# Gates of a gated hybrid block, projected in other pairs of column tiles and in another order among the pool's products

## The chip, the cores and the metric

One core of one Trainium2 chip runs the whole block: one decoder layer for a sequence of 1024 tokens of width 1024, in float32. The metric is the device time of one execution in microseconds, as the median of several runs. The profile is one more execution, recorded by the hardware profiler; its times count from the start of its span.

## The reference

```python
proj = x @ w_in            # 1024 x 1024 @ 1024 x 7168
q, f_pre, i_val, o_gate, pool_v, gate_a, gate_b = jnp.split(proj, ...)   # 1024 columns each
o = hgrn2_chunked(...)     # recurrence, 8 heads of 128
a = (rmsnorm(o) * g * sigmoid(o_gate)) @ w_a
b = (causal means of pool_v over 2, 4, 8, 16 tokens, minus pool_v) @ w_pool, in 4 groups of 256, * pool_scale
mix = (sigmoid(gate_a) * a + sigmoid(gate_b) * b) @ w_out
x = LN(alpha * x + mix);  x = LN(alpha * x + relu(x @ w_up)^2 @ w_down)
```

The change concerns the two projections gate_a and gate_b (columns 5 x 1024 and 6 x 1024 of w_in), their sigmoids, and the products of the pool, b.

## The kernel before

**Products.** The big products are made by a Strassen-like scheme. `pair` (L260) takes two column tiles of 128 columns of a weight matrix, each in an upper and a lower half of 512 rows: blocks b11 and b21 of the first column tile, b12 and b22 of the second. It makes the outputs of both column tiles for both halves of the tokens by seven products instead of eight. Each weight operand is split in a high and a low part (`split`, L117 on ScalarE, L118 on VectorE) and each of the seven products consists of twelve matmuls of 128 x 128 by 128 x 512 (L199 to L201: four blocks of rows, high times high, high times low, low times high). The products sum in three PSUM banks: p1 in the first, copied to SBUF (L268, tile c11) before p6, p5 and p3 go on in the same bank; p2 in the second; p7 and p4 in the third. The copies and sums (L268, L272) yield four results of 128 x 512: first column tile and first token half at p7, then the others at p5, p4 and p3. Each result is handed to a `take` function.

**Weights.** `w_blocks` (L206) fetches the blocks into two raw tiles, one for each half of the rows, of which there are two buffers in all: a pair fills both. If the second column tile directly follows the first in the matrix, a single DMA for each raw tile fetches 256 neighbouring columns, in rows of 1 KB (L214). Otherwise there is one DMA for each block, in rows of 512 bytes (L220).

**Tiles of the results.** `c_soon` hands out tiles of a ring with two buffers (c11, short-lived), `c_late` tiles of a ring with four (c21, c22 and the tile of the last sum). `c_tile()` of `o_sums` takes every third of its tiles from the first ring and the others from the second. A tile becomes free when the DMA that stores it has landed.

**The order of the work around the change.** For each head h and token half u there is a call of `hgrn` (L803), the recurrence, and around it the pairs that project the next heads' inputs and the output gates. A table, `EXTRAS` (L933), places further work behind each (h, u):

- `pooled(g)`: projection and causal means of pool group g, stored to DRAM (heads 0 to 3);
- `gates(j)` (L685): one pair of column tile j of gate_a and column tile j of gate_b, 1024 columns apart; a sigmoid on each of the four results (L693), each stored to DRAM (L696) as ga[j] and gb[j] for both halves of the tokens. The last, gates(7), uses the room tiles q, f, og and v instead of the two rings, since those have no user any more, and multiplies (L695) its two results for gate_b with the pool's products pb[7], which it loads, before it stores them as pb[7];
- `o_sums(kp)` (L602): loads four tiles of the normed recurrence outputs o (L591), adds and subtracts them (L605 to L608) and stores four sums (L610). They are operands of the merge. o_sums(3) is called with tiles of its own at the end of the last `hgrn`;
- `pool_products(g)` (L705): loads the group's weights (L713), four pooled tiles and the gates gb of its two column tiles, splits the weights and pooled tiles, makes 24 matmuls (L104 to L106), scales and gates the results out of PSUM on VectorE (L726) and stores them as pb (L727). For column tile 7 the gate isn't there yet; ScalarE scales the result alone (L724). Its tiles are ten room tiles: three q, three f, two og and two v, which is all of these rings; its weights take one of the two raw buffers.

Before, the table says for heads 4 to 7: gates(0) behind (4, 1); gates(1), o_sums(0) behind (5, 1); gates(2), o_sums(1) behind (6, 1); gates(3) behind (7, 0); and behind (7, 1) gates(4), o_sums(2), pool_products(0), gates(5), pool_products(1), gates(6), pool_products(2), pool_products(3), gates(7). The last `hgrn` runs at a raised priority.

Behind that comes the merge: `o_operand` (L594) loads o and the sums, pairs of w_a make a, and `gated` (L982) loads ga and pb and forms the gated sum.

The source's order isn't yet the order on the chip: a scheduler with a model of the time line (`schedule_with_timeline_sim=True`) lays out each engine's instructions at build, by the source's order, priorities and free tiles. Afterwards each engine works its list in order. All the DMAs named here are issued by SyncE (SP), also in order: an issue that waits for its tile or its data holds up those behind it.

Of the kernel before, what the change touches and what calls it, by code (L numbers as in the profile page):

```python
# [42 lines left out]
def tile_hybrid_block(  # L43
# [77 lines left out]
    def split_into(t, src):  # L121
# [9 lines left out]
        out=cmask, in_=cmask, compare_op=ALU.is_ge, fill=0.0, base=0,  # L131
# [93 lines left out]
    def loaded_blocks(*args):  # L225
        raw, load = w_blocks(*args)
        load(0, 1)
        return raw
# [20 lines left out]
    spare = []  # L249
# [7 lines left out]
    def c_late():  # L257
        return c_tile(False)
# [95 lines left out]
    def run(*pairs, made=(), behind=()):  # L354


        for i, steps in enumerate(zip(*pairs)):
            made_now = list(made[i]) if made else []
            if made_now:
                made_now.pop(0)()  # L360
            with tc.issue_after(made_last[behind[i]]) if behind and behind[i] else nullcontext():
                ws = [{operand: operand() for operand in operands} for operands, _ in steps]
            for n in range(len(ws[0])):
                if made_now:
                    made_now.pop(0)()
# [223 lines left out]
    def loaded(src, tile_of):  # L589
        t = tile_of()  # L590
        nc.sync.dma_start(out=t, in_=src)  # L591
        return t
# [22 lines left out]
    with tc.tile_pool(name="tmp", bufs=1, side="right", reuse_waits="tile") as tmp:  # L615
# [14 lines left out]
        def tt(tag, dtype=F32):  # L630
            pool = tmp if tag in ("q", "f", "og", "v") else hgp
            return pool.tile([P, HALF], dtype, tag=tag, name=nm(tag), bufs=RINGS.get(tag, 1))
# [35 lines left out]
            src = vd[u][h // CH].rearrange("p (c d) -> p c d", d=HALF)[:, :, h % CH * P : (h % CH + 1) * P]  # L668
            return loaded(src, lambda: tmp.tile([P, CH, P], F32, tag="v", name=nm("v"), bufs=RINGS["v"]))

        def output_gates(h):

            def take(dst, src=False):
                def put(t):
                    s = c_late() if src else t
                    A.activation(s, t, AF.Sigmoid)
                    nc.sync.dma_start(out=dst, in_=s)
                return put

            run(pair(  # L680
                loaded_blocks(w_in, 3 * D + h * P, 3 * D + (h + 1) * P), (c_soon, c_late, c_late),
                (take(ogd[h][0]), take(ogd[h + 1][0], True), take(ogd[h][1]), take(ogd[h + 1][1])),
            ))

        def gates(j):  # L685
            spare = j == KT - 1
            rooms = [lambda tag=tag: tt(tag) for tag in ("q", "f", "og")] if spare else (c_soon, c_late, c_late)

            def take(dst, src=None, more=None):
                def put(t):  # L690
                    s = (tt("v") if spare else c_late()) if src else t
                    more_of = loaded(more, lambda: tt("v")) if more is not None else None
                    A.activation(s, t, AF.Sigmoid)  # L693
                    if more_of is not None:
                        V.tensor_mul(s, s, more_of)  # L695
                    nc.sync.dma_start(out=dst if more is None else more, in_=s)  # L696
                return put

            more = pbd[j] if spare else (None, None)
            run(pair(  # L700
                loaded_blocks(w_in, 5 * D + j * P, 6 * D + j * P), rooms,
                (take(gad[j][0]), take(gbd[j][0], True, more[0]), take(gad[j][1]), take(gbd[j][1], False, more[1])),
            ))

        def pool_products(g):  # L705

            tags = iter(("q", "f", "og", "v") * 3)

            def room(dtype=F32):
                return tt(next(tags), dtype)  # L710

            raw = raw_tile().rearrange("p k n c -> p (k n c)")[:, : 2 * 2 * P].rearrange("p (k c) -> p k c", c=2 * P)
            nc.sync.dma_start(out=raw, in_=w_pool[g].rearrange("(k p) c -> p k c", p=P))  # L713
            wh, wl = split(raw, lambda: room(F32R).rearrange("p (k c) -> p k c", c=2 * P))
            for u in range(2):
                pl = [split(loaded(pod[2 * g + i][u], room), row_tile) for i in range(2)]
                for i in range(2):
                    w = slice(i * P, (i + 1) * P)
                    j = 2 * g + i
                    t = room() if j == KT - 1 else loaded(gbd[j][u], room)  # L720
                    ps = ps_tile()
                    mm3(ps, [(wh[:, c, w], wl[:, c, w], *pl[c]) for c in range(2)])
                    if j == KT - 1:
                        A.activation(t, ps, AF.Copy, scale=pscale[:, j : j + 1])  # L724
                    else:
                        V.scalar_tensor_tensor(t, ps, pscale[:, j : j + 1], t, ALU.mult, ALU.mult)  # L726
                    nc.sync.dma_start(out=pbd[j][u], in_=t)  # L727

        def pooled(g):
# [73 lines left out]
        def hgrn(h, u, ft, q, v, og, state):  # L803
# [139 lines left out]
        for h in range(HEADS):  # L943
            fs, qs = nxt
            state = None
            for u in range(2):
                v, og = values(h, u), loaded(ogd[h][u], lambda: tt("og"))
                with tc.high_priority(PRIO_LAST) if (h, u) == (HEADS - 1, 1) else nullcontext():
                    state = hgrn(h, u, fs[u], qs[u], v, og, state)
                    if (h, u) == (HEADS - 1, 1):  # L950
                        tags = iter(("tD", "tE", "tF", "tC"))
                        o_sums(h - CH, lambda: tt(next(tags)))
                if h + 1 < HEADS and u:
                    nxt = head_inputs(h + 1)
                    if h % 2:
                        output_gates(h + 1)
                for what, j in EXTRAS.get((h, u), ()):
                    dict(gates=gates, pooled=pooled, pool_products=pool_products, o_sums=o_sums)[what](j)


        hg_scope.close()
# [436 lines left out]
```

## Time and profile before

| | |
|---|---|
| median of 3 runs | 1461.44 us (1459.88 to 1463.6) |
| the profiled execution, its own time | 1460.58 us |
| its span | 1458.8 us |
| PE (matmuls) busy | 1437.8 us, 99% |
| VectorE, ScalarE busy | 1138.1 us, 754.6 us |
| mean rate of the DMAs | 155 GB/s |

PE stands for TensorE's matmuls and PEld for its weight loads, DVE for VectorE, ACT for ScalarE, SPq for the queue of SyncE. A group or an instruction is named by its line, its engine, its operation, and `out<-in` by the program's tile names: `ga<-c` stores a result tile as ga, `q<-gb` loads a gate into a room tile. A bracket behind an instruction of the timeline holds the idle time of its engine before it and what ended that.

### The profile page before, as it was taken

How to read it: one execution, taken by the hardware profiler on the slowest of the kernel's cores; microseconds unless marked ns; L12 is line 12 of the kernel's file. 1: busy time of each engine (PE TensorE's matmuls, PEld its weight loads, DVE VectorE, ACT ScalarE, POOL GpSimd, SP SyncE). 2: the span in 40 equal slices, each digit the busy share in tenths (PEclk: the TensorE clock that was granted, in tenths of full speed). 3: DMA queues.
4: the chain of work that ended last, by engine and by line, in shares of the span. 5: the costliest groups of instructions: out<-in, count | busy, mean ns of one | idle time of the engine just before them, and what ended most of it. 6: DMA issues, size and time to landing. Idle time of an engine off the chain costs nothing.

```text
span 1458.8 us, 20894 instructions
## 1 busy us (share of the span) xinstructions
PE 1437.8 (99%) x7505; PEld 1183.8 (81%) x7505; DVE 1138.1 (78%) x1838; ACT 754.6 (52%) x1383; POOL 65.6 (4%) x244
## 2 busy tenths in 40 slices
PE   9999999999999999999999999999999999999997
PEld 7888888887888888777888878888888888888886
DVE  5967989899998795768985597666666787777977
ACT  5445566565556566355442376555555443433535
POOL 0002010011000020000002100000000100000000
PEclk9999999999999999999999999999999999999999
DMA  7242233323233547987563235445464874444422
GB/s 253 66 130 87 88 102 102 94 88 109 95 109 109 172 126 238 345 289 248 197 223 119 73 96 193 154 139 169 143 242 152 285 261 146 158 146 158 130 73 116
DMA packets 160616, 226.84 MB, mean 155 GB/s; under 512 B 11232, under 2 KB 84480, under 8 KB 160512
## 3 DMA queue, kind: packets, MB, share of 16 engines
q1 hardware_dynamic: 158576, 218.93, 44.9%
q0 software_dynamic: 1152, 4.19, 0.8%
q10 hardware_dynamic: 784, 2.38, 0.6%
q8 instruction: 59, 0.97, 0.3%
q14 instruction: 45, 0.37, 0.1%
HBM read 154.16 MB, written 71.30 MB: 155 GB/s over the span
## 4 chain that ended last, share of the span: by engine, by line
PE 87%; DVE 5%; DMA 4%; ACT 2%; issue 1%; SPq 0%; DVEq 0%; ACTq 0%
PE ps_pj L199 15%; PE ps_pj L201 14%; PE ps_pj L200 14%; PE ps_pj L1280 4%; PE ps_pj L1281 4%; PE ps_pj L1279 4%; PE ps_pj L104 2%; PE ps_pj L105 2%; PE ps_pj L106 2%; PE ps_tr L1279 1%; PE ps_tr L1281 1%; PE ps_tr L1280 1%; DMA raw<-in_w_in_dram 1%; PE sc L887 1%; PE ps_sc L199 1%
## 5 line engine op out<-in xcount | busy, mean ns | idle before, releaser
L199 PE MATMUL ps_pj<-act,w 128*128 128x512 f32 x1068 | 419.6, 395 | 5.9 <-ACT c L268 3.6
L200 PE MATMUL ps_pj<-act,w 128*128 128x512 f32 x1068 | 416.8, 391 | 0.5 <-DVE act L123 0.5
L201 PE MATMUL ps_pj<-act,w 128*128 128x512 f32 x1068 | 412.5, 392 | 0.1
L199 PEld LDWEIGHTS ps_pj<-act,w 128*128 128x128 f32 x1068 | 200.5, 188 | 51.4 <-ACT c L268 5.1
L201 PEld LDWEIGHTS ps_pj<-act,w 128*128 128x128 f32 x1068 | 200.5, 188 | 42.9 <-DVE w L118 1.1
L200 PEld LDWEIGHTS ps_pj<-act,w 128*128 128x128 f32 x1068 | 200.6, 188 | 40.9 <-DVE act L123 0.9
L117 ACT CAST w<-t 128x512 fp32r<-128x512 f32 x170 | 104.8, 620 | 111.4 <-PE ps_pj L200 50.1
L118 DVE TENSOR_TENSOR w<-raw,w 128x512 fp32r<-128x512 f32 x143 | 99.4, 701 | 57.0 <-ACT w L117 42.2
L117 ACT CAST w<-raw 128x512 fp32r<-128x512 f32 x143 | 88.3, 620 | 96.3 <-PE ps_pj L200 44.5
L118 DVE TENSOR_TENSOR w<-t,w 128x512 fp32r<-128x512 f32 x170 | 116.3, 688 | 23.7 <-ACT w L117 21.8
L1241 ACT CAST act<-act 128x1024 fp32r<-128x1024 f32 x66 | 67.1, 1050 | 107.2 <-issue 35.0
L1280 PE MATMUL ps_pj<-act,act 128*128 128x512 f32 x240 | 93.3, 390 | 0.2 <-DVE act L1242 0.2
L1281 PE MATMUL ps_pj<-act,act 128*128 128x512 f32 x240 | 93.1, 389 | 0.0
L1279 PE MATMUL ps_pj<-act,act 128*128 128x512 f32 x240 | 92.4, 389 | 0.0
L1242 DVE TENSOR_TENSOR act<-act,act 128x1024 fp32r<-128x1024 f32 x66 | 79.4, 1221 | 15.9 <-ACT act L1241 15.9
L272 DVE TENSOR_TENSOR c<-c,ps_pj 128x512 f32<-128x512 f32 x95 | 64.8, 683 | 31.0 <-PE ps_pj L201 23.9
L268 ACT COPY c<-ps_pj 128x512 f32<-128x512 f32 x96 | 55.4, 584 | 10.3 <-PE ps_pj L201 7.7
L814 DVE RECIPROCAL tC<-tA 128x128 f32<-128x128 f32 x64 | 54.7, 913 | 0.0
L1280 PEld LDWEIGHTS ps_pj<-act,act 128*128 128x128 f32 x240 | 45.0, 188 | 10.0 <-DVE act L1242 0.6
L1281 PEld LDWEIGHTS ps_pj<-act,act 128*128 128x128 f32 x240 | 45.0, 188 | 9.4
L1279 PEld LDWEIGHTS ps_pj<-act,act 128*128 128x128 f32 x240 | 45.0, 188 | 9.3
L238 DVE TENSOR_TENSOR t<-raw,raw 128x512 f32<-128x512 f32 x43 | 29.6, 689 | 23.5 <-DMA raw<-in_w_in_dram 20.7
(415 smaller groups left out, 2728.4 us busy)
## 6 DMA issues: line engine op xcount, KB each, us to landing
h<-c SPq DMA_DIRECT2D x106, 256.0 KB, 2.3
act<-h SPq DMA_DIRECT2D x78, 256.0 KB, 3.0
raw<-in_w_in_dram SPq DMA_DIRECT2D x64, 256.0 KB, 3.5
draw<-in_w_down_dram SPq DMA_DIRECT2D x16, 1024.0 KB, 8.4
raw<-in_w_up_dram SPq DMA_DIRECT2D x30, 512.0 KB, 4.1
raw<-in_w_in_dram SPq DMA_DIRECT2D x18, 512.0 KB, 3.9
hf<-h SPq DMA_DIRECT2D x34, 256.0 KB, 3.0
c<-o SPq DMA_DIRECT2D x24, 256.0 KB, 3.9
```

Source lines behind the costliest of these rows:

```text
L117: A.copy(hi, src)
L118: V.tensor_sub(lo, src, f(hi))
L199: PE.matmul(ps, wh[:, k], th, start=first and k == 0, stop=False, skip_group_check=True)
L200: PE.matmul(ps, wh[:, k], tl, start=False, stop=False, skip_group_check=True)
L201: PE.matmul(ps, wl[:, k], th, start=False, stop=k == CH - 1, skip_group_check=True)
L268: A.copy(t, ps)
L272: V.tensor_add(t, t, ps)
L1241: A.copy(hi, src)
L1242: V.tensor_sub(lo, src, f(hi))
L1279: PE.matmul(ps, hh[:, w], wh, start=fresh and n == 0, stop=False, skip_group_check=True)
L1280: PE.matmul(ps, hh[:, w], wl, start=False, stop=False, skip_group_check=True)
L1281: PE.matmul(ps, hl[:, w], wh, start=False, stop=n == M - 1, skip_group_check=True)
```

## The change

`gates(j)` is replaced by `mix_gates(i)`, one pair of the column tiles 2i and 2i + 1 of gate_a, and `pool_gates(i)`, the same of gate_b. Both, and `output_gates`, call a common `gate_pair`; the column tiles of a pair are now neighbours, so L214's single DMA serves each raw tile. The four results get their sigmoid and are stored; only mix_gates(3) uses the room tiles. All of gate_b is projected by the four pool_gates behind heads 4 to 7, so pool_products loads a gate for each column tile, scales and gates all on VectorE, and the multiplication behind the last pair is gone. o_sums(2) moves from (7, 1) to (7, 0), and the order behind (7, 1) is new.

```diff
-        def output_gates(h):
+        def gate_pair(col, dst, rooms=None):
+
+            c11, c21, c22, s12 = rooms or (c_soon, c_late, c_late, c_late)
 
             def take(dst, src=False):
                 def put(t):
-                    s = c_late() if src else t
+                    s = s12() if src else t
                     A.activation(s, t, AF.Sigmoid)
                     nc.sync.dma_start(out=dst, in_=s)
                 return put
 
             run(pair(
-                loaded_blocks(w_in, 3 * D + h * P, 3 * D + (h + 1) * P), (c_soon, c_late, c_late),
-                (take(ogd[h][0]), take(ogd[h + 1][0], True), take(ogd[h][1]), take(ogd[h + 1][1])),
+                loaded_blocks(w_in, col, col + P), (c11, c21, c22),
+                (take(dst[0][0]), take(dst[1][0], True), take(dst[0][1]), take(dst[1][1])),
             ))
 
-        def gates(j):
...
-            run(pair(
-                loaded_blocks(w_in, 5 * D + j * P, 6 * D + j * P), rooms,
-                (take(gad[j][0]), take(gbd[j][0], True, more[0]), take(gad[j][1]), take(gbd[j][1], False, more[1])),
-            ))
+        def output_gates(h):
+            gate_pair(3 * D + h * P, ogd[h : h + 2])
+
+        def mix_gates(i):
+            gate_pair(
+                5 * D + 2 * i * P, gad[2 * i : 2 * i + 2],
+                [lambda tag=tag: tt(tag) for tag in ("q", "f", "og", "v")] if i == HEADS // 2 - 1 else None,
+            )
+
+        def pool_gates(i):
+            gate_pair(6 * D + 2 * i * P, gbd[2 * i : 2 * i + 2])
 
         def pool_products(g):
...
-                    t = room() if j == KT - 1 else loaded(gbd[j][u], room)
+                    t = loaded(gbd[j][u], room)
                     ps = ps_tile()
                     mm3(ps, [(wh[:, c, w], wl[:, c, w], *pl[c]) for c in range(2)])
-                    if j == KT - 1:
-                        A.activation(t, ps, AF.Copy, scale=pscale[:, j : j + 1])
-                    else:
-                        V.scalar_tensor_tensor(t, ps, pscale[:, j : j + 1], t, ALU.mult, ALU.mult)
+                    V.scalar_tensor_tensor(t, ps, pscale[:, j : j + 1], t, ALU.mult, ALU.mult)
                     nc.sync.dma_start(out=pbd[j][u], in_=t)
...
-        EXTRAS[4, 1] = (("gates", 0),)
-        EXTRAS[5, 1] = ("gates", 1), ("o_sums", 0)
-        EXTRAS[6, 1] = ("gates", 2), ("o_sums", 1)
-        EXTRAS[7, 0] = (("gates", 3),)
-        EXTRAS[7, 1] = (
-            ("gates", 4), ("o_sums", 2), ("pool_products", 0), ("gates", 5), ("pool_products", 1), ("gates", 6), ("pool_products", 2), ("pool_products", 3), ("gates", 7),
-        )
+        EXTRAS[4, 1] = (("pool_gates", 0),)
+        EXTRAS[5, 1] = (("pool_gates", 1), ("o_sums", 0))
+        EXTRAS[6, 1] = (("pool_gates", 2), ("o_sums", 1))
+        EXTRAS[7, 0] = (("pool_gates", 3), ("o_sums", 2))
+        EXTRAS[7, 1] = (("mix_gates", 0), ("mix_gates", 1), ("pool_products", 0), ("pool_products", 1), ("mix_gates", 2), ("pool_products", 2), ("pool_products", 3), ("mix_gates", 3))
```

More of the change, by code (lines that the diff above doesn't have):

```diff
@@ L680, in output_gates @@
             run(pair(
-                loaded_blocks(w_in, 3 * D + h * P, 3 * D + (h + 1) * P), (c_soon, c_late, c_late),
-                (take(ogd[h][0]), take(ogd[h + 1][0], True), take(ogd[h][1]), take(ogd[h + 1][1])),
-            ))
-        def gates(j):
[L686 to L699, printed above, removed]
-            run(pair(
-                loaded_blocks(w_in, 5 * D + j * P, 6 * D + j * P), rooms,
-                (take(gad[j][0]), take(gbd[j][0], True, more[0]), take(gad[j][1]), take(gbd[j][1], False, more[1])),
-            ))
+                loaded_blocks(w_in, col, col + P), (c11, c21, c22),
+                (take(dst[0][0]), take(dst[1][0], True), take(dst[0][1]), take(dst[1][1])),
+            ))
+        def output_gates(h):
[7 more added lines that the diff above has]
+            gate_pair(6 * D + 2 * i * P, gbd[2 * i : 2 * i + 2])
         def pool_products(g):
@@ L957, in tile_hybrid_block @@
                 for what, j in EXTRAS.get((h, u), ()):
-                    dict(gates=gates, pooled=pooled, pool_products=pool_products, o_sums=o_sums)[what](j)
+                    dict(
+                        mix_gates=mix_gates, pool_gates=pool_gates, pooled=pooled, pool_products=pool_products, o_sums=o_sums,
+                    )[what](j)
         hg_scope.close()
```

## The prediction

> **What bounds the kernel now.** I read the page's first two parts, then busy time by stretches, then the idle intervals of PE. From the page:
>
> ```profile
> span 1458.8 us, 20894 instructions
> ...
> PE 1437.8 (99%) x7505; PEld 1183.8 (81%) x7505; DVE 1138.1 (78%) x1838; ACT 754.6 (52%) x1383; POOL 65.6 (4%) x244
> ...
> PE   9999999999999999999999999999999999999997
> ...
> DMA  7242233323233547987563235445464874444422
> ```
>
> PE is busy for 1437.8 of 1458.8 us, so no other engine's work is worth anything unless it ends an idle interval of PE. The change moves no product and adds none: eight pairs of seven products before, eight after, and the same 96 of the pool. So the time can only change by what PE waits. The DMA row says where waits may be made: slices 16 to 19 (547 to 693 us) are the fullest, and the edited stretch, from the end of the recurrence to the start of the merge, lies there. The view of stretches:
>
> ```profile
> 545.00:690.00 145.00, 139.99 (x686) 112.99 (x685) 100.29 (x162) 77.87 (x152) 0.00 (x0) 1.00 0.83 276
> 690.00:845.00 155.00, 155.00 (x708) 128.33 (x707) 115.82 (x192) 60.83 (x105) 14.41 (x6) 1.00 0.48 161
> 590.00:600.00 10.00, 7.36 (x31) 5.15 (x29) 9.99 (x17) 5.30 (x10) 0.00 (x0) 1.00 1.04 387
> 610.00:620.00 10.00, 10.00 (x45) 8.26 (x44) 9.04 (x15) 4.09 (x7) 0.00 (x0) 1.00 1.03 366
> ```
>
> The columns are length, then PE, PEld, DVE, ACT, POOL, the granted clock (1.00), the DMA engines' busy share and GB/s. From 545 to 690 us PE is idle for 145.00 - 139.99 = 5.0 us. PE's ends are modelled, so I take the weight loads as a second count: in the full stretch behind, PEld is busy 128.33 / 155 = 0.828 of the time; 145 us at that share would be 120.0, the row has 112.99, and 7.0 / 0.828 = 8.5 us are missing. The most that this change can gain is thus 5.0 to 8.5 us, 0.3 to 0.6% of the run. [...]
>
> The idle intervals themselves, from the timeline of PE (start, duration, and in brackets the idle time with what ended it):
>
> ```profile
> 595.97 0.50 PE L199 MATMUL ps_pj<-act,w 128*128 128x512 f32 x1 [2.45 <-ACT c L268]
> 599.20 0.73 PE L104 MATMUL ps_pj<-w,q 128*128 128x512 f32 x2 [0.19 <-ACT w L117]
> ...
> 642.84 0.39 PE L104 MATMUL ps_pj<-w,q 128*128 128x512 f32 x1
> 643.06 0.39 PE L105 MATMUL ps_pj<-w,q 128*128 128x512 f32 x1
> ...
> 644.35 0.50 PE L199 MATMUL ps_pj<-act,w 128*128 128x512 f32 x1 [0.68 <-ACT f L724]
> 656.29 0.50 PE L199 MATMUL ps_pj<-act,w 128*128 128x512 f32 x1 [0.74 <-ACT w L117]
> ...
> 683.05 0.50 PE L199 MATMUL ps_hg<-act,w 128*128 128x512 f32 x1 [0.51 <-ACT room L268]
> ```
>
> Products start 0.22 to 0.23 us apart when nothing is late (642.84, 643.06). After a wait the first takes 0.50 instead of 0.39, so a wait costs its idle time and 0.11: 2.56, 0.30, 0.79, 0.85 and 0.62 us for the five, 5.1 together. Half of it is one wait.
>
> **Part 1: o_sums(2) moves from behind the fifth gate pair to behind the fourth.** The wait at 595.97 is its work. First p1 of the sixth pair had to be copied out of its bank (L268) before p6 could go on in that bank, and the copy needed a tile that o_sums(2) held:
>
> ```profile
> 595.34 0.59 ACT L268 COPY c<-ps_pj 128x512 f32<-128x512 f32 x1 [2.13 <-DMA s<-c]
> ```
>
> SP's own timeline shows why those tiles were held so long:
>
> ```profile
> 557.44 0.38 SPq L591 DMA_DIRECT2D c<-o  x1
> ...
> 572.93 0.32 SPq L591 DMA_DIRECT2D c<-o  x1
> ...
> 580.51 0.32 SPq L929 DMA_DIRECT2D o<-og  x1
> 583.44 0.32 SPq L591 DMA_DIRECT2D tC<-o  x1
> ...
> 584.76 1.01 SPq L591 DMA_DIRECT2D c<-o  x2
> ...
> 590.73 0.32 SPq L610 DMA_DIRECT2D s<-c  x1
> ```
>
> Of its four loads (c<-o) the first goes out at 557.44 and takes a short-lived tile; the last two leave at 584.76, behind tC<-o, which stood in SP's queue until the last head's output (580.51) had landed at 583.4. The first sum is stored at 590.73, and 595.34 is that landing. Placed behind the fourth pair, the loads are ahead of all that in SP's queue. But now the fifth pair (the first of the gates of a) is the next user of the two short-lived tiles. When would it get one? Before, o_sums(1) gives its tiles back when its stores have landed, and these rows bound the rest:
>
> ```profile
> 551.21 0.45 SPq L610 DMA_DIRECT2D s<-c  x1
> ...
> c<-o SPq DMA_DIRECT2D x24, 256.0 KB, 3.9
> s<-c SPq DMA_DIRECT2D x12, 256.0 KB, 4.2
> ...
> 556.90 0.57 ACT L268 COPY c<-ps_pj 128x512 f32<-128x512 f32 x1
> ...
> 564.78 0.39 PE L199 MATMUL ps_pj<-act,w 128*128 128x512 f32 x1
> ```
>
> The last store goes at 551.21 and lands some 4.2 us later, at 555.4; then a load (3.9), the first sum (0.7, the length of the other DVE adds here) and its store (4.2): the tile is free at about 564.2, and the copy ends 0.6 later, at 564.8. In the run before, this copy was made at 556.90, but what needs it, p6 of that pair, starts only at 564.78 (twelve products at 0.227 behind p1 and the small products of the last head). So the earlier place just fits: 0 if the loads are issued at once, and if SP, whose queue also holds the four stores of the pair and the loads of the last head, delays them as it did at 584.76, up to the old 2.56. I take 0.5, since the head-of-line block at 583.44 is behind it. Part 1: -2.56 + 0.5 = **-2.1 us**, between -2.6 and 0.
>
> **Part 2: pool_products 0 and 1 side by side.** Before, a gate pair stood between them; after, they run like 2 and 3 did, in front of a pair. What that costs is the wait at 644.35:
>
> ```profile
> 643.09 0.62 ACT L117 CAST w<-raw 128x512 fp32r<-128x512 f32 x1 [4.38 <-DMA raw<-in_w_in_dram]
> ```
>
> The next pair's second half of weights had to wait for the raw tile that the pool's weights held, and ACT stood behind it for 4.38 us, the copy out of the bank too. I copy that price: **+0.8 us**. Its bounds are 0 (if the pair in front still has products to lie beside it) and the price of the third rival. The small wait at 599.20, a cast for pool_products(1) just behind the long wait, goes with it: **-0.2**, between -0.3 and 0. The pair 2 and 3 keeps its own 0.79: the copy at L724 only changes engine, from one in-order queue that waits for the raw tile to another (the low half of the same weights, on DVE).
>
> **Part 3: the last pair.** Before, it multiplied two of its results with the pool's; the loads, multiplications and copies:
>
> ```profile
> L695 DVE TENSOR_TENSOR og<-og,v 128x512 f32<-128x512 f32 x1 | 0.7, 687 | 0.0
> L724 ACT ACTIVATE f<-ps_pj,prm 128x512 f32<-128x512 f32 x2 | 1.4, 684 | 0.0
> L726 DVE SCALAR_TENSOR_TENSOR q<-ps_pj,prm,q 128x512 f32<-128x512 f32 x8 | 6.0, 748 | 0.3 <-PE ps_pj L106 0.2
> ...
> 649.27 0.93 SPq L591 DMA_DIRECT2D v<-pb  x2
> ...
> 655.10 0.62 ACT L122 CAST act<-c 128x512 fp32r<-128x512 f32 x1 [1.58 <-DMA c<-o]
> ```
>
> DVE loses two multiplications of 0.69 and gains two scalings of 0.75: +0.1, hidden, with DVE idle for 44.7 of the 145 us. ACT loses 2 x 0.68. On SP the two loads v<-pb (0.93 us of issue) go, which stood ahead of the load whose landing ACT waited for at 655.10; PE's wait at 656.29 is two casts behind it. Two loads of gate tiles come instead, some 9 us sooner. And the last store no longer waits for a multiplication (0.69), so the merge's first loads in SP's queue go out that much sooner; the wait at 683.05 hangs on those. Together **-0.7 us**, between 0 and -(0.85 + 0.62) = -1.5.
>
> **Part 4: rows of 1 KB.** Four loads of 256 KB become two of 512 KB in each pair:
>
> ```profile
> raw<-in_w_in_dram SPq DMA_DIRECT2D x64, 256.0 KB, 3.5
> ...
> raw<-in_w_in_dram SPq DMA_DIRECT2D x18, 512.0 KB, 3.9
> ```
>
> The first product's weights arrive 0.4 us later (3.9 against 3.5), all of a pair's together sooner, by two issues of about 0.4 us. They are fetched during the pair ahead, whose products cover it; without that cover 0.4 us a pair, 3.2 in all, and as much the other way. In the first three pairs, up to 545 us, PE idles 0.2 us in all from 400 on, so nothing can be gained there. I take 0.
>
> **Sum.** -2.1 + 0.8 - 0.2 - 0.7 = -2.2 us. The profiled execution took 1460.58 us (span 1458.8 and 1.8 around it): 1458.4. It lies 0.9 under the median of the runs, 1461.44; against that median **1459.2 us**, 0.15% less. About 0.3% (4.4 us, below 1457.1 or above 1465.8) is what a measurement of this kernel tells from no change.
>
> **Rivals.** (a) *Nearly all waits go*: the lighter queue also frees 599.20, 644.35, 656.29 and 683.05, and the new neighbourhood of the pool costs nothing. 5.1 to 8.5 us less: 1453 to 1456, middle 1454.6. For it: each wait ends in a landing or a queue, and DMA share is above 1.0 there. Against: the bytes stay the same.
> (b) *The long wait only moves*: the fifth pair waits for o_sums(2)'s tiles as the sixth did, 0 for part 1 and for 599.20, +0.8 and -0.7: 1461.5. For it: my margin above is nil. Against: the old delay came from SP's queue at 583.
> (c) *Slower: the pool's transfers become the bound.* Each pool_products moves 13 tiles of 256 KB: its weights, four pooled tiles, four gates, four results, 3.41 MB. At the 366 GB/s of the 610 to 620 row that is 9.3 us; its 24 products take 24 x 0.227 = 5.4. Two side by side: 18.6 against 10.9, 7.7 us short, as ten room tiles hold just one call's transfers. It decides if the first one's tiles aren't loaded before the fifth and sixth pair's products end. In place of +0.8 that makes 1459.2 - 0.8 + 7.7 = 1466.1, and up to 1468 with (b). For it: 1.03 DMA share. Against: 2 and 3 stood side by side and cost 0.79.
>
> **Chances.** Forecast 0.42, (a) 0.18, (b) 0.20, (c) 0.20. The range leaves out the lower half of (a) and the upper part of (c): 1455.0 to 1466.5. Faster by over 0.3%: all of (a) and a little of the forecast, 0.20; slower: most of (c), 0.15; within: 0.65.
>
> **What would show it.** Right: no wait of over 1 us at L199 behind the copy of L268 between 545 and 610; the four c<-o of o_sums(2) within about 5 us of each other, before 565; a wait of about 0.8 in front of the third pair of a's gates; no v<-pb. Wrong: a wait of several us near 565 (b), or a DMA share above 1 with gaps between L104 to L106 around 600 (c). A scheduler that puts the instructions in another order than the source could upset any of these.

## The result, and the profile after

The kernel after took 1464.16 us (median of 22 runs, 1459.59 to 1468.21), the kernel before, run beside it, 1460.49 us (22 runs, 1458.52 to 1463.6). The ratio is 1.0022, 95% interval 1.0015 to 1.0029: the change makes the kernel slower by 0.2%, where a gain of 0.15% was forecast. That is within the 0.3% that the prediction called no change, and within its range, but on the other side.

The profiled execution is one of the quickest of the 22: 1460.01 us, span 1458.3. What the page says of it, the totals of the engines and the DMA row of the 40 slices:

```profile
span 1458.3 us, 20886 instructions
...
PE 1436.5 (99%) x7505; PEld 1184.3 (81%) x7505; DVE 1136.9 (78%) x1838; ACT 754.8 (52%) x1381; POOL 64.9 (4%) x244
...
DMA  7232233323233546987662235445464874444422
```

All is as before: as many products, PE busy for 99%, the same two dense places for the DMAs. The stretches, with the columns of before:

```profile
545.00:690.00 145.00, 138.29 (x652) 112.83 (x646) 100.04 (x160) 77.17 (x149) 0.00 (x0) 1.00 0.82 276
...
590.00:600.00 10.00, 10.00 (x46) 8.29 (x45) 3.36 (x5) 3.99 (x7) 0.00 (x0) 1.00 1.08 376
610.00:620.00 10.00, 8.78 (x40) 6.96 (x39) 6.70 (x11) 3.12 (x6) 0.00 (x0) 1.00 0.98 351
```

In the edited stretch PE is idle for 145.00 - 138.29 = 6.7 us instead of 5.0. Around 590, where before had its long wait, PE now works without a break (10.00 of 10), at a DMA share of 1.08; around 610 a wait has come. PE's timeline after has these idle intervals of 0.2 us and more:

```profile
554.08 0.50 PE L199 MATMUL ps_pj<-act,w 128*128 128x512 f32 x1 [0.75 <-ACT c L268]
...
568.43 0.49 PE L902 MATMUL ps_hg<-v,att 128*128 128x128 f32 x2 [2.16 <-DVE st L874]
...
613.32 0.47 PE L199 MATMUL ps_pj<-act,w 128*128 128x512 f32 x1 [1.22 <-DVE q L717]
...
645.86 0.47 PE L199 MATMUL ps_pj<-act,w 128*128 128x512 f32 x1 [2.02 <-DVE q L717]
...
681.76 0.51 PE L199 MATMUL ps_pj<-act,w 128*128 128x512 f32 x1 [0.28 <-ACT w L117]
...
682.77 0.50 PE L199 MATMUL ps_hg<-act,w 128*128 128x512 f32 x1 [0.21 <-ACT room L268]
```

(Lines have shifted by up to nine: L902 and L874 are the recurrence, L717 the scaling by the gate, L678 and L679 the sigmoid and its store.) The waits at 596, 599 and 656 are gone. New are those at 554, 568 and 613; the one of 0.68 at 644 has become 2.02.

**The wait at 568** is o_sums(2) in its new place. SP and VectorE, in that order:

```profile
552.82 0.32 SPq L591 DMA_DIRECT2D c<-o  x1
...
560.19 0.32 SPq L920 DMA_DIRECT2D o<-og  x1
561.45 0.32 SPq L679 DMA_DIRECT2D gb<-c  x1
562.57 0.32 SPq L591 DMA_DIRECT2D tF<-o  x1
...
563.41 0.90 SPq L591 DMA_DIRECT2D c<-o  x2
```

```profile
567.42 0.69 DVE L605 TENSOR_TENSOR c<-c,c 128x512 f32<-128x512 f32 x1 [3.79 <-DMA c<-o]
568.03 0.34 DVE L874 SCALAR_TENSOR_TENSOR st<-st,dec,ps_hg 128x128 f32<-128x128 f32 x1
```

Two of o_sums(2)'s four loads leave only at 563.41 and 563.93. They come behind two stores of the fourth pair (gb<-c) and behind tF<-o, which reads what o<-og had stored at 560.19. Their own tiles no longer held them: by the semaphores in the trace, one waits for o_sums(1)'s last store, which had landed by 554.7, and the other for a result of the fourth pair, landed by 559.8. So the first sum stands at the head of VectorE's queue for 3.79 us, with the state update L874 of the last head behind it, and PE's product L902 behind that. It is the same kind of block in SP's queue as before, one step of the recurrence earlier, and now an engine that the recurrence needs waits behind it.

The wait at 554 is that for a copy (L268) which stands in ScalarE's queue behind a cast of weights; that cast waited 5.02 us for its load:

```profile
550.28 0.62 ACT L117 CAST w<-raw 128x512 fp32r<-128x512 f32 x1 [5.02 <-DMA raw<-in_w_in_dram]
```

**The waits at 613 and 646** are those of the scaling L717, which frees the PSUM bank that the next pair's products need. VectorE at the one place and at the other, and SP's issue of the gate of the second:

```profile
612.42 0.75 DVE L717 SCALAR_TENSOR_TENSOR q<-ps_pj,prm,q 128x512 f32<-128x512 f32 x1 [3.30 <-DMA q<-gb]
...
640.84 0.69 DVE L238 TENSOR_TENSOR t<-raw,raw 128x512 f32<-128x512 f32 x1 [0.58 <-DMA raw<-in_w_in_dram]
...
643.37 0.69 DVE L281 TENSOR_TENSOR t<-t,raw 128x512 f32<-128x512 f32 x1
644.96 0.75 DVE L717 SCALAR_TENSOR_TENSOR q<-ps_pj,prm,q 128x512 f32<-128x512 f32 x1 [0.90 <-DMA q<-gb]
```

```profile
639.14 0.44 SPq L718 DMA_DIRECT2D pb<-q  x1
639.67 0.42 SPq L591 DMA_DIRECT2D q<-gb  x1
```

At 613 the scaling waits for its gate alone, whose load took 5.8 us. At 646 two things come together: in VectorE's queue the scaling stands behind five splits and sums of the next pair (640.84 to 644.06), which had to wait for that pair's weights; and its gate, asked for only at 639.67, isn't there for 0.90 us more. Column tile 7 had neither before: its copy L724 needed no gate, and on ScalarE stood behind one cast (643.09).

**A second profile of each.** The unchanged kernels, profiled once more, show how much these waits vary (the first row is the kernel before, the others the kernel after; 545 to 690 us, and a piece of it):

```profile
545.00:690.00 145.00, 141.59 (x696) 114.68 (x695) 102.32 (x165) 79.07 (x154) 0.00 (x0) 1.00 0.84 281
```

```profile
545.00:690.00 145.00, 136.38 (x664) 110.24 (x665) 96.74 (x155) 75.09 (x145) 0.00 (x0) 0.99 0.80 264
650.00:653.40 3.40, 3.40 (x10) 2.63 (x9) 3.40 (x6) 2.07 (x4) 0.00 (x0) 0.50 0.95 322
```

PE is idle for 5.0 and 3.4 us before, 6.7 and 8.6 after: 3.5 us more on the mean of two, near the 3.7 between the medians. A second count goes by the products: between the 4000th and the 3300th matmul from the end (546.15 and 705.70 us in the first profile of before) all four executions make the same ones. They take 159.55 and 157.85 us before, 160.20 and 164.50 after. So the stretch itself is longer after the change, by 0.65 us in the first pair of profiles and 6.65 in the second. The second profile of after, whose own time was 1465.26 us, shows one thing more, a granted clock of 0.50 for 3.4 us behind a longer wait at the same place. PE's timeline there:

```profile
648.89 0.47 PE L199 MATMUL ps_pj<-act,w 128*128 128x512 f32 x1 [3.12 <-DVE q L717]
...
650.62 0.63 PE L199 MATMUL ps_pj<-act,w 128*128 128x512 f32 x1
651.04 0.63 PE L200 MATMUL ps_pj<-act,w 128*128 128x512 f32 x1
```

Products 0.42 us apart instead of 0.22 to 0.23: half of the 3.4 us, 1.7, is lost on top of the wait. VectorE shows what made the wait longer:

```profile
644.71 0.69 DVE L238 TENSOR_TENSOR t<-raw,raw 128x512 f32<-128x512 f32 x1 [2.59 <-DMA raw<-in_w_in_dram]
...
647.99 0.75 DVE L717 SCALAR_TENSOR_TENSOR q<-ps_pj,prm,q 128x512 f32<-128x512 f32 x1
```

Here the five splits and sums, whose weights came 3.9 us later than in the first profile, end at 647.93, and the gate, asked for at 641.36, lands 6.6 us later, at 647.97: the queue and the gate each held the scaling until then.

### The profile page after: what moved, and what is told of

Read it like the earlier page. It is cut to its first block, busy times and chain, and to the rows that moved or that the text cites. A ratio compares the mean times of both kernels' runs of the same rounds, so it can differ in the third digit from the quotient of the medians.

```text
span 1458.3 us, 20886 instructions
## 1 busy us (share of the span) xinstructions
PE 1436.5 (99%) x7505; PEld 1184.3 (81%) x7505; DVE 1136.9 (78%) x1838; ACT 754.8 (52%) x1381; POOL 64.9 (4%) x244
## 4 chain that ended last, share of the span: by engine, by line
PE 91%; DMA 4%; DVE 2%; issue 1%; ACT 1%; SPq 0%; DVEq 0%; ACTq 0%
PE ps_pj L199 16%; PE ps_pj L201 16%; PE ps_pj L200 16%; PE ps_pj L1271 4%; PE ps_pj L1272 4%; PE ps_pj L1270 4%; PE ps_pj L105 2%; PE ps_pj L104 2%; PE ps_pj L106 2%; PE sc L878 1%; PE ps_tr L1271 1%; PE ps_tr L1272 1%; PE ps_tr L1270 1%; PE ps_sc L199 1%; PE ps_hg L199 1%
## 5 line engine op out<-in xcount | busy, mean ns | idle before, releaser
L268 ACT COPY c<-ps_pj 128x512 f32<-128x512 f32 x96 | 55.5, 585 | 10.4 <-PE ps_pj L201 6.6
```

The source lines that it names most:

```text
L268: A.copy(t, ps)
```

## The experiments

Theory: the change removes the wait at 596 but makes two of 2 to 3 us, at 568 by o_sums(2) and at 646 by the gates that VectorE scales with, long enough to bring the half clock at times, as in the second profile (0.50 behind 3.12 us). Rivals: the pool's transfers are the bound, however the work is ordered; the new place of o_sums(2) alone is the loss; or the difference is only that of single executions. For each edit the scheduler lays out the whole program anew, so an experiment changes more than its diff says; the readings rest on the waits in its trace as much as on its time. Ratios are to the kernel before, run beside it.

**The kernel after once more (x1).**

> The changed kernel itself, unchanged, to get more executions and another profile. Clock theory: the loss is not in the waits (their sum in the profiled execution is no larger than before) but in the granted TensorE clock, which a wait of about 2 us can drop to a half for a few us. Then a run's time goes with its mean clock, about 1.5 us for each 0.001; the median is again 3 to 4 us above the kernel before at a mean clock near 0.996 against 0.998, and if this profile is one of the slower executions it has a slice with a clock below 1.0 just behind one of the waits at 554, 568, 613 or 646 us. Rival, waits: the waits differ from run to run; then a slower profile shows longer idle intervals at full clock, and the mean clock does not follow the time.

1463.96 us against 1461.54, ratio 1.0015 (1.0004 to 1.0027). The loss is confirmed, and its size varies: 2.4 us here, 3.7 in the result. Here the runs can be compared at equal mean granted clock: at 0.997 the kernel after took 1463.9 (6 runs), the kernel before 1461.6 (10 runs). So 2.3 us are lost at the same clock. The mean clock itself was 0.9968 against 0.9973, which at 1.5 us for 0.001 (last section) is 0.8 us. So the loss is not the clock's alone, as the expectation's theory had it; the waits are the larger part.

**o_sums(2) back behind the fifth pair, in the changed kernel (x2); and o_sums(2) alone moved forward, in the kernel before (x4).**

```diff
-        EXTRAS[7, 0] = (("pool_gates", 3), ("o_sums", 2))
-        EXTRAS[7, 1] = (("mix_gates", 0), ("mix_gates", 1), ...
+        EXTRAS[7, 0] = (("pool_gates", 3),)
+        EXTRAS[7, 1] = (("mix_gates", 0), ("o_sums", 2), ("mix_gates", 1), ...
```

> The changed kernel with o_sums(2) back behind the first pair of (7, 1). If the early o_sums(2) makes the wait of 2.2 us at 568 (and the 0.75 at 554), both go, a wait near 596 may come back, and by the clock theory the median moves with the largest single wait that is left: 1461 to 1464 if the one at 646 (2.0 us) stays. By the waits theory about 2.5 us less than the changed kernel, if the wait near 596 doesn't come back, and nothing if it does.

```diff
-        EXTRAS[7, 0] = (("gates", 3),)
+        EXTRAS[7, 0] = (("gates", 3), ("o_sums", 2))
-            ("gates", 4), ("o_sums", 2), ("pool_products", 0), ...
+            ("gates", 4), ("pool_products", 0), ...
```

> The kernel before with o_sums(2) alone moved behind the fourth pair, as in the change. If the early o_sums(2) makes the wait at 568, it is here too, and the old 2.45 us at 596 is gone: idle time as before, and by the waits theory the same time as before (within 1 us). By the clock theory the time depends on how often the one long wait drops the clock: within 2 us of before either way.

1470.15 us, 1.0053 (1.0037 to 1.0070), and 1467.68 us, 1.0038 (1.0024 to 1.0053). The first and the last of PE's four waits over 1 us from 545 to 700 us (total, times, longest), of the one and then of the other:

```profile
PE ps_pj L199 <- DVE q L717: 3.9, 1, 3.9
...
PE ps_pj L199 <- ACT w L117: 2.8, 1, 2.8
```

```profile
PE ps_pj L104 <- ACT w L117: 2.1, 1, 2.1
...
PE ps_pj L199 <- ACT w L117: 1.4, 1, 1.4
```

With o_sums(2) back, the waits at 554 and 568 are gone; but three others of 2.8 to 3.5 us come in, at 591 to 622, and the one for the scaling L717 grows to 3.9. In the kernel before, the same move costs 0.38% by itself. The wait at 568 that was expected there doesn't appear; instead PE waits 2.1, 1.5 and 1.8 us, at 572 to 577, for the pool's first operands and a copy out of a bank (L268). Much of both losses is half clock behind these waits:

```profile
545.00:700.00 155.00, 141.26 (x639) 114.78 (x632) 98.36 (x158) 75.62 (x147) 0.00 (x0) 0.94 0.76 252
```

This is x2, with a mean clock of 0.94 between 545 and 700 us. The half clock lasts 17.1 us there, and PE works in 12.0 of them, so 6.0 are lost; in x4 it is 2.4, in the second profile of the kernel after 1.7. So the move forward loses about 6 us in the one order (1467.68 against some 1461.5) and saves about 6 in the other (1470.15 against 1463.96). The terms of the change don't add up one by one, and neither edit came out in the range that was expected.

**The pool's calls apart (x3).**

```diff
-... ("mix_gates", 1), ("pool_products", 0), ("pool_products", 1), ("mix_gates", 2), ...
+... ("pool_products", 0), ("mix_gates", 1), ("pool_products", 1), ("mix_gates", 2), ...
```

> The changed kernel with pool_products(0) ahead of the second pair of (7, 1) instead of behind it, so that 0 and 1 aren't neighbours. The wait of 1.2 us at 613 should go; those at 568 and 646 stay. By the waits theory 1.2 us less than the changed kernel. By the clock theory nothing or up to 2 us less, since the two waits of 2 us are still there.

1472.63 us, 1.0074 (1.0060 to 1.0089). Its longest wait is the first call's, for its first operands, split on ScalarE at 574.38:

```profile
PE ps_pj L104 <- ACT w L117: 5.8, 1, 5.8
```

Moving them apart in this way costs 9 us more. But the first call comes one pair sooner in this order, when its tiles aren't there yet, so the edit doesn't show what the neighbourhood alone costs. The waits at 568 and 646, which were expected to stay, are gone as well. For 568 the order on VectorE tells why: here the first sum waits 2.95 us too (570.65), but stands behind the last L874 (565.99) and not ahead of it.

**Other tiles for the gates of the pool (w1, y1, y4).** In the changed kernel, with the other tiles as they were:

```diff
-                    t = loaded(gbd[j][u], room)
+                    t = loaded(gbd[j][u], (lambda: (next(tags), c_late())[1]) if g in (3,) else room)
```

> As y1, without the flaw that y1 had: there the pooled tiles of the second token half moved from the rings og and v to q and f, and PE then waited 3.5 us for those. Here only the four gate tiles of the last pool group are in the c ring; all the other tiles keep their rings. Gate theory: the wait at 646 (bank held until the gate lands) goes below 1 us, no half clock there, 1460 to 1462. Transfer theory: the transfers of pool_products(3) as a whole are late, and another wait of 2 us or more stands between 640 and 650: 1463 or more.

1461.52 us, 1.0016 (1.0007 to 1.0025); idle from 545 to 690 us 6.6. PE's three longest waits, and VectorE's last scaling of the first token half:

```profile
PE ps_hg L902 <- DVE st L874: 2.5, 1, 2.5
PE ps_pj L199 <- ACT w L117: 1.2, 1, 1.2
PE ps_pj L199 <- ACT c L268: 1.0, 1, 1.0
```

```profile
642.58 0.75 DVE L717 SCALAR_TENSOR_TENSOR c<-ps_pj,prm,c 128x512 f32<-128x512 f32 x1 [0.31 <-PE ps_pj L106]
645.74 0.69 DVE L238 TENSOR_TENSOR t<-raw,raw 128x512 f32<-128x512 f32 x1 [2.41 <-DMA raw<-in_w_in_dram]
```

With the gate in time, the scaling is laid ahead of the splits that wait for the weights, and the wait at 646 is gone. 1.2 and 0.8 us come in its place at 657 and 659, behind the next weights and the next copy. The median is the lowest of all edits of the kernel after, but by the ratio no gain over that kernel is shown, as the intervals overlap.

Two forms of the same idea were worse. With ring tiles for the last call's gates but the room tiles handed on, so that those of other operands changed too:

```diff
-                    t = loaded(gbd[j][u], room)
+                    t = loaded(gbd[j][u], c_late if g == 3 else room)
```

> The changed kernel, but the gate tiles of the last pool group (pool_products(3)) go into the ring of c tiles, which is free by then, in place of the room tiles. Gate theory: PE's wait at 646 to 649 (2.0 and 3.1 us in the two profiles) is for a bank that the scaling on VectorE holds until the gate's load has landed, and that load can't be issued until a room tile is free. Then the wait falls below 1 us, no half clock follows there, and the time falls by 2 to 4 us, to 1460 to 1462. Rival, transfers: the load lands as late as before because the DMA engines are full (share 0.95 in that stretch); then wait and time stay.

1467.64 us, 1.0048 (1.0031 to 1.0066). And with ring tiles for all gates of the pool (`c_late` in every call):

> As the run before, with the gate tiles of all four pool groups in the c ring. Gate theory: the wait of 1.1 to 1.2 us at 613 goes too, another 1 us. Against it: the ring is also that of the gate pairs' results, so that a copy out of a bank (L268) may wait for it; then a wait of 1 to 3 us at L268 appears between 585 and 630 and the time is no better than in the run before.

1466.81 us, 1.0043 (1.0029 to 1.0057): four waits of the pool's own products for the scaling of earlier ones (L717, 5.1 us together) replace the next pairs' waits for it. This profile shows no half clock between 545 and 690 (clock 1.00 there) and yet 1467.89 us, so the waits alone can make such a time.

**The sums of o_sums(2) on GpSimd (w2)**, to take them out of VectorE's queue:

```diff
-        V.tensor_add(a22, a21, a22)
+        E = G if kp == 2 else V
+        E.tensor_add(a22, a21, a22)
```

(and the other three alike)

> The changed kernel with the four adds and subtractions of o_sums(2) on GpSimd, so that they don't stand in VectorE's queue ahead of the last head's scan while their load is under way. If that queue makes the wait at 568 (2.2 to 3.1 us in five profiles), it goes below 0.7 us, and with it its half clocks: 1460 to 1462. If the wait is the scan's own or the transfers', it stays and so does the time (1464).

1465.67 us, 1.0041 (1.0028 to 1.0054). No wait behind L874 is left. The other profiles agree that the order in VectorE's queue makes that wait: the five in which the first sum stands ahead of the last L874 (two of the kernel after, w1, y1, y4) have it, with 2.2 to 3.1 us; x3, x4, y3, v1 and v2, in which the sum stands behind it, don't, though the sum waits 3 to 5 us there as well. In the place of the wait behind L874, ScalarE holds the fifth pair's first copy, for a tile that the sums keep:

```profile
574.50 0.59 ACT L268 COPY c<-ps_pj 128x512 f32<-128x512 f32 x1 [4.11 <-POOL c L608]
```

**Both edits together (w3)**, those of w1 and w2.

> The two edits together (gate tiles of the last group in the c ring, sums of o_sums(2) on GpSimd). If both waits come from what the two theories say, the stretch keeps the wait at 613 and little else, idle time under 4 us against 5.0 of the kernel before, with nothing over 2 us: 1457 to 1460, faster than both kernels. If they only move: 1463 or more.

1464.11 us, 1.0031 (1.0019 to 1.0043). One wait over 0.6 us is left, PE's 3.1 us at 573 (with 3.4 us at half clock behind it), and it is the same copy:

```profile
572.34 0.59 ACT L268 COPY c<-ps_pj 128x512 f32<-128x512 f32 x1 [3.97 <-DMA s<-c]
```

This is rival (b) of the prediction: the fifth pair waits for o_sums(2)'s stores. The profile is of the quickest of the five runs (1460.86 us), so it doesn't show what made the others slower. With both waits gone the time was expected below that of the kernel before; it is above.

**The kernel after, w1 and w3 with the tiles of o_sums(2) from the ring of four alone (v1, v2, v3)**, so that this copy doesn't share them:

```diff
     def o_sums(kp, tile_of=c_tile):
+        tile_of = c_late if kp == 2 else tile_of
```

> The changed kernel with the four tiles of o_sums(2) from the ring of four alone. Theory (the loads of o_sums(2) are late because one of them shares the short ring, or the tiles of the fourth pair are stored late in SP's queue): if the short ring is what counts, the copy of L268 near 554 and the wait near 568 go and the run comes to 1461 to 1462. Rival (the long ring is the scarcer: the fourth pair, o_sums(2) and the fifth pair now ask for eleven tiles of it in a row): a wait of 3 us or more near 570, 1466 or above.

> The same with the gate tiles of the last pool call in the ring of results as well. Theory: what the first of these four gains, less the wait at 646 of 2 us and its half clock: 1459 to 1461. Rival: the wait near 570 of the long ring stays, 1464 or above.

> Sums on GpSimd, gate tiles of the last pool call in the ring of results, and the tiles of o_sums(2) from the ring of four alone. Theory: the single wait that the kernel with both cures had, 3.1 us at 573 behind the copy of the fifth pair, was the short ring's; without it no wait over 1.5 us is left between 545 and 700, the clock stays whole, and the run takes 1456 to 1458, less than both kernels. Rival: the wait is that of the long ring or of SP's queue and stays; 1463 to 1466.

1468.60 us, 1.0060 (1.0046 to 1.0074); 1467.78, 1.0045 (1.0031 to 1.0059); 1468.70, 1.0058 (1.0045 to 1.0071). PE's wait for the last head's state and that for the fifth pair's copy are in none of the three, and each is slower than the kernel that it was made from. In their place PE waits for the next pair's weights, 2.2 to 4.1 us together between 574 and 580, and from 611 to 613 for the pool's operands, as in these two rows of the second:

```profile
577.40 0.50 PE L201 MATMUL ps_pj<-act,w 128*128 128x512 f32 x1 [1.28 <-DVE w L118]
...
611.74 0.80 PE L104 MATMUL ps_pj<-w,q 128*128 128x512 f32 x1 [4.11 <-ACT q L117]
```

So the last wait of w3 goes with the short ring, as the theory had it, but nothing is won by its going. The times are those of the rivals or above (v3 was to take 1466 at most), but by waits for transfers and not, as the rivals said, for the ring.

**o_sums(2) one pair sooner still (w6)**, behind o_sums(1):

```diff
-        EXTRAS[6, 1] = (("pool_gates", 2), ("o_sums", 1))
-        EXTRAS[7, 0] = (("pool_gates", 3), ("o_sums", 2))
+        EXTRAS[6, 1] = (("pool_gates", 2), ("o_sums", 1), ("o_sums", 2))
+        EXTRAS[7, 0] = (("pool_gates", 3),)
```

> The changed kernel with o_sums(2) directly behind o_sums(1), one gate pair earlier still. If what matters is that its loads and sums are out of the way of the last head, the waits at 554 and 568 go: 1460 to 1462. If the ring of c tiles is what matters, the fourth gate pair now waits for its tiles (L268, around 545): 1464 or more.

1468.73 us, 1.0062 (1.0050 to 1.0074). Its longest wait, 3.9 us at 551, is in the recurrence; a wait for a copy (L268), which was expected near 545, comes at 561 with 2.5 us.

**Rows of 512 bytes for the new pairs (y3).**

```diff
+            apart = src is w_in and c1 >= 5 * D
-                if c2 == c1 + P and len(which) == 2:
+                if c2 == c1 + P and len(which) == 2 and not apart:
```

> The changed kernel, but the weights of all its new gate pairs come in four loads with rows of 512 bytes, as before the change. If the form of these loads is worth nothing, as forecast, the time stays within 1 us of the changed kernel (1464). Rival: the rows of 1 KB relieve the full DMA engines, and without them the waits between 545 and 700 grow: 1466 or more.

1469.25 us, 1.0063 (1.0047 to 1.0079), above the interval of the kernel after: with two DMAs in rows of 512 bytes in place of one in rows of 1 KB it takes some 5 us more. The longest wait is for the fifth pair's copy again, at 572.48,

```profile
572.48 0.58 ACT L269 COPY c<-ps_pj 128x512 f32<-128x512 f32 x1 [6.13 <-DMA s<-c]
```

6.1 us behind a store of o_sums(2). How much of the 5 us is the rows and how much the scheduler's other layout isn't separated; half clock behind the waits lasts 13.7 us in this profile, and PE works in 12.5 of them, so 6.2 are lost by it.

**Waits of known length (z1)**, alone on the chip: the whole block is left out (the output is a copy of x). PE makes 96 chains of 48 products, and between them waits for a chain of copies on ScalarE.

> No part of the block is computed (the output is a copy of x). 96 groups of 48 matmuls of 128x512, and behind each a chain of copies on ScalarE on which the next group's weights depend, of 16 lengths from about 0.5 to 4 us, six times each. [...]

Two rows of its timeline and two of its stretches:

```profile
305.10 11.17 PE L37 MATMUL ps<-xs,w 128*128 128x512 f32 x48 [1.67 <-ACT w L48]
...
599.64 12.82 PE L37 MATMUL ps<-xs,w 128*128 128x512 f32 x48 [2.64 <-ACT w L48]
```

```profile
305.10:308.50 3.40, 3.40 (x15) 2.82 (x16) 0.00 (x0) 0.00 (x0) 1.00 0.00 0
...
331.10:334.50 3.40, 3.40 (x9) 2.67 (x10) 0.00 (x0) 0.00 (x0) 0.56 0.02 5
```

48 products take 11.17 us behind a wait of 1.67 us and 1.65 us more behind 2.64; behind one of 2.00 us, at 331.10, the clock is 0.56. Over all 96 waits, those followed by a half clock:

| wait, us | 0.7 | 1.0 | 1.3 | 1.7 | 2.0 | 2.3 | 2.6 | 3.0 | 3.3 | 3.6 | 4.3 |
|---|---|---|---|---|---|---|---|---|---|---|---|
| halved | 0 of 6 | 0 of 12 | 0 of 6 | 0 of 12 | 2 of 6 | 3 of 12 | 4 of 6 | 9 of 12 | 5 of 6 | 8 of 12 | 5 of 5 |

(One wait more, of 14 us at the start, is left out.) So behind waits of 1.7 us or less the clock was never halved here (0 of 36), and behind those of 2 to 3.6 us in 31 of 54 cases, in 8 of 12 at 3.6.

**The kernel before once more (b1).**

> The kernel before, unchanged, for another profile of it. If its waits are the same in every execution, the wait near 596 is 2 to 3 us again and PE idles 5 to 6 us from 545 to 700; the theory that the changed kernel loses by waits that vary from run to run and by the half clock asks that the mean granted clock of these runs lies above that of the changed kernel's (0.997 to 0.998 against 0.996 to 0.997). Rival: the clock of both is the same, and the difference is the waits alone.

1460.41 us, 0.9997 (0.9988 to 1.0006). Its waits:

```profile
PE ps_pj L199 <- ACT c L268: 1.1, 1, 1.1
...
PE ps_pj L199 <- ACT f L724: 0.6, 1, 0.6
```

Its other waits are as they were. The long one, at 594 here, on which part 1 of the prediction stood, is 1.1 us instead of 2.4. Its runs had a mean clock of 0.9978.

## Why the prediction was wrong

**The bound: right.** PE is busy for 99% in both, and what the traces show in the edited stretch is PE's waits, and half clock behind some of them. The ceiling of a gain, 5.0 us of idle time in the one profile at hand, is 3.4 in the second one.

**Part 1 failed**, in the step "So the earlier place just fits: 0 if the loads are issued at once ... I take 0.5, since the head-of-line block at 583.44 is behind it". The loads were reckoned from the landing of o_sums(1)'s stores, as if nothing stood between. A tile was indeed free by 554.7, near the 555.4 of the prediction, but the load into it left at 563.41: SP's queue held it behind stores of the fourth pair and a block of the recurrence. The block at 583.44 was not the only one of its kind; the step before it has one too (o<-og, then tF<-o), at 560 to 563, and the new place is behind that. And the price asked for the wrong waiter: not the fifth pair's copy but the sum itself was late, and behind it in VectorE's queue stood the recurrence. With 0.11 for each first product, as in the prediction, the two new waits cost (0.75 + 0.11) + (2.16 + 0.11) = 3.1, the old one gave back 2.56: +0.6 instead of -2.1. Of this the 2.3 at 568 are shown to be the sum's, by the order on VectorE. The 0.9 at 554 go with o_sums(2) in x2, but y1, with o_sums(2) as early, doesn't have them either.

**Part 2: near in size, not in mechanism.** Between the pool's second call and the next pair 1.22 + 0.11 = 1.3 us are lost at 613 instead of 0.8, and 599.20 gave back 0.3. But the waiter isn't the pair's weights behind the raw tile, as copied from 644.35; it is the scaling without its gate (3.30 us idle on VectorE, for a load of 5.8 us).

"The pair 2 and 3 keeps its own 0.79: the copy at L724 only changes engine" **failed**. It changes its inputs (a gate that must first be loaded) and its neighbours in the queue (five instructions behind the same late weights instead of one). 2.02 instead of 0.68 in this profile, 3.12 and a half clock in the next: +1.3 or more instead of 0. w1, with other tiles for that gate, has no such wait, but waits of 1.2 and 0.8 us behind it.

**Part 3: right in both profiles of the kernel after.** The loads v<-pb are gone, and so is the wait at 656; the wait of 0.51 at 683 is now 0.28 + 0.21 in two. 0.74 + 0.11 = 0.85 saved, forecast 0.7. That these loads alone made it isn't shown: w1 and y4, without them too, wait 1.2 and 1.3 us there, at 657 and 663.

**Part 4: not borne out by y3.** The rows of 1 KB were put at nothing; the kernel after without them takes about 5 us more. The term had asked only whether the weights come in time, not whom the four loads hold up in a full queue. As far as these 5 us are the rows', the gain is in the result, and the rest of the change costs the more.

**The sum.** 0.6 + 1.3 - 0.3 + 1.3 - 0.9 = +2.0 us of waits in the first profile, where -2.2 was forecast. Idle time is not a full count of it: by the prediction's second count, the weight loads, (112.99 - 112.83) / 0.828 = 0.2 us were lost, and by the products 0.65. That this execution was still 0.6 us below the profiled one of before comes from outside the stretch: it had come there, at the product of 546.15 us, 1.05 us ahead. It was a quick one, and no proof of a gain; in the second profiles the stretch loses 6.65 us. The prediction rested on a single profile whose waits vary by 1 to 2 us, about as much as the change was forecast to be worth. That the median fell inside the range is therefore no sign that the forecast held: the sign was wrong.

**No term for the clock.** The granted clock of 1.00 in the rows was taken as given. At equal clock 2.3 us were lost, by the clock some 0.8.

**Rivals.** (a) failed. (b) didn't happen in the kernel after, but does in w2, w3 and y3. (c), the slower side, came out near in time (1466.1), by luck: between the pool's products at 590 to 600 us there is no gap at a DMA share of 1.08. Nor were the gates late by slower transfers: those at 613 and 646 took 5.8 and 5.3 us to land, and before the median of such loads was 5.1. A slower result by waits that move was not among the rivals.

**What stays open.** No edit beat the kernel before, and w3, with the two largest new waits gone, still takes 0.3% more: those two are shown to come from the change, but not to be the whole of its loss. Why the same move of o_sums(2) saves in one order and costs in the other was not taken apart; the traces say only that each time another user of the rings, of the room tiles or of SP's queue comes late, and that half clock behind the longer waits adds to it.

## What to carry to other kernels

Where the idle time of the edited stretch is 0.3% of the run, a step that is moved can move a wait rather than remove it, as in every edit here. Before pricing it at the old wait, list who holds its tiles and what stands ahead of it in the DMA queue at the new place, and what stands behind it on its engine. When an operation changes engine, compare its inputs, not only its time. And take two profiles before a term of 2 us is believed: here the wait that carried the forecast was 2.4 us in one execution and 1.1 in another.

## What the runs showed of the hardware

In the second profile of the kernel after (x1) the granted clock was 0.50 for 3.4 us, from 650.0 to 653.4, behind a wait of 3.12 us; in x2 it was 0.94 on the mean of 545 to 700 us. In z1 a half clock followed waits as short as 2.0 us (2 of 6); no wait of up to 1.7 us had it (0 of 36), waits of 2.6 us had it in 4 of 6 cases, and those of 3.6 us not always (8 of 12). Where PE worked throughout such 3.4 us, they cost about 1.7 us (1.65 in z1 behind 2.64 us). Against the run's 1464 us that is 0.0012 of its mean clock, so 1.5 us for 0.001, an estimate; the 22 runs of the kernel after go roughly by that: 1460.0 us at a mean clock of 0.999 (2 runs), 1463.7 at 0.997 (6), 1466.2 at 0.995 (4). The waits go with it, so not all of that is the clock; the one run at 0.994 took 1464.6.
